# A hybrid decoder layer on one core: the second half of the sample's mLSTM states, moved from the mLSTM stage to VectorE's work beside the MLP

## The chip, the core and the metric

The kernel runs on 1 core of one Trainium2 chip. A time is device microseconds (us) of one execution; three runs were made of the kernel before, with a median of 2251.63 us (2251.58 to 2252.29).

## The reference, cut to what matters

One layer for 256 prompt tokens and 64 sample tokens (8 sequences of 8 tokens), all in fp32, with a width of 2048. Two token mixers read one input projection: an mLSTM with 4 heads (keys of 256, values of 512) and an HGRN2 recurrence with 8 heads. They are merged by gates, projected, normalised, and followed by an MLP of width 8192.

```python
h, C, n, m = _mlstm(q, k, v, ig, lf, C0, n0, m0)     # 4 heads, state C (256 x 512) each
...
mix = merged @ w_out
x1 = layernorm(alpha * x + mix)
hid = square(relu(x1 @ w_up))                        # 2048 -> 8192
y  = layernorm(alpha * x1 + hid @ w_down)            # 8192 -> 2048
```

Inside the mLSTM, each of the 8 sample sequences of each head brings a state of 256x512 and gives back a new one. The old state is also read by the queries:

```python
num   = einsum('bhts,bhsv->bhtv', s, v) + w_inter * einsum('bhtk,bhkv->bhtv', q, C)
w_end = exp(b[-1] - b + ig - m_new)
decay = exp(b[-1] + m - m_new)
C_new = decay * C + einsum('bhs,bhsk,bhsv->bhkv', w_end, k, v)
```

So a new state is the old one times one number (its sequence's decay) plus eight outer products, one for each token. A state's 256 rows are held as two halves of 128; the second half is what this change is about. The prompt's own states (one per head, from zero) are a different piece, computed at the very end.

## The kernel before, in words

**Weights.** Every large product is written as three products of halves: a factor is split into a high part (`xh`, `wh`) and the rest (`xl`, `wl`), both in the reduced fp32 form that TensorE reads, and xh·wh, xl·wh and xh·wl are added in a PSUM bank. There are 304 weight tiles of 128 output columns, each 16 steps of 128 input rows: 14,592 matmuls that take a 128x128 weight block and move 320 tokens past it. The tiles come in this order: 4 mLSTM heads (values, keys, queries), 8 HGRN heads, the output gates, the branch projections, the output projection `wo`, and then the MLP, four times 16 tiles of the up projection (`up`) and 16 of the down projection (`dn`).

**Units.** A unit is half a tile: 8 steps, 24 matmuls, 128x1024 weights (512 KB). Its way to TensorE has four links. `reload` (L527) issues the load on SP's DMA queue into one of three raw buffers `wr`. `prep` (L488) has ScalarE copy the high half (`A`, L342), into a free pair of buffers `wh`, `wl`. `low_half` (L515) has VectorE subtract it (L520), and spawns the load of the unit three further on into the same raw buffer. `give` (L601) takes the pair back when the unit's last matmul has been issued. There are three pairs `wh`, `wl`; from `wo` on to the end five wide pairs in the tile `bb` (`self.wx`) come to them, so eight in the MLP.

**Order of the side work.** Everything beside the weights is written as chains (Python generators) that ask for one instruction at a time, wait for events, or take and return buffers of a pool. `Sched` (L152) keeps an estimated time for each engine and steps the chains in the order of their priorities each time that a weight step has been placed (`pump`). An instruction is written when its chain's estimate is no more than 300 ns ahead of TensorE's; on ScalarE and VectorE the engine's own estimate must also be within 900 ns, and side matmuls are let in up to 900 ns at a time. The result is a fixed order for each engine; each engine then runs its own in order.

**The states before.** `m_states` (L1403) loads, for each head, 16 tiles of 128x512 (256 KB each): both halves of 8 sequences, in groups of four tiles, from a pool of 14 buffers `cb`, which are carved from other tiles of the stage (`rx`, `f` and others). `m_sample` (L1256) has two waves per head, each of four sequences with both halves, so eight tiles: the queries' product with the old states (eight matmuls, "q·C" below), and the outer products of the first half (`m_sums`, L1423: four matmuls `ra` of 32 rows by 512, one for each sequence, into four banks). `m_update` (L1432) then has VectorE form state times decay plus bank (L1441), spawns the stores, has TensorE make the second half's four sums into the same banks, and updates the second half. K and V for it come from `kst` and `vst`, copies of the sample's rows laid out in four blocks of 32 rows (`fourfold`, L1126, which reads K back from DRAM, 256 columns).

**The end.** `m_C` (L1194) computes the prompt's states from K and V that are loaded again from DRAM by POOL's queue. For heads 0 and 1 these go to buffers that `give` has set aside; for heads 2 and 3 (`late`) they go to the raw weight buffers `wr` once the last low half is done (`rest_ev`, L525), and are split by ScalarE (L342) and VectorE (L1918) into halves again. Meanwhile the last tile of the down projection is added by VectorE (L2240, L2241), and goes through the last layer norm's sums (L2065, L2066; earlier tiles L2053, L2054). TensorE adds these over rows by 24 matmuls of one column each, and multiplies the m_C halves before and after them.

## Time and profile before

| | before |
|---|---|
| time, median of 3 runs | 2251.63 us (2251.58 to 2252.29) |
| span of the profiled execution | 2246.3 us |
| TensorE (PE) busy | 2240.6 us, 16,218 matmul records |
| VectorE (DVE) busy | 1445.7 us, 64% |
| ScalarE (ACT) busy | 1012.3 us, 45% |
| GpSimd (POOL) busy | 21.0 us, 1% |
| DMA | 432.56 MB, mean 193 GB/s |

The profile is one execution of the kernel on the chip. The span goes from its first to its last instruction; the run's time has some 5 us around it. A row of an engine says what was busy; "idle before" is the time in which that engine stood still just ahead of an instruction, with the engine and the tile whose end released it. The PE row counts matmuls as busy while one is in the pipeline, so that 310 ns matmuls which start every 146 ns make an engine that is 100% busy. PEclk is the clock that TensorE was granted; it stands at 1.00 here. In rows of the timeline the first number is the start in us, the second the duration in us from the first to the last of a group ("x4").

### The profile page before, as it was taken

The page shows a single profiled execution, that of the slowest core. Times are in us where ns is not written, and L with a number is a line of the kernel's source. Part 1 is how long each engine was busy: PE and PEld are TensorE (multiplying, and loading weights), DVE is VectorE, ACT ScalarE, POOL GpSimd, SP SyncE. Part 2 cuts the span into 40 slices and gives each one's busy share as a digit, 9 for nine tenths or more (in the row PEclk, how much of TensorE's full clock was granted, in tenths as well). Part 3 has the DMA queues.
Part 4 walks back from the last instruction along what each step waited for, and adds up shares of the span by engine and source line. Part 5 has one row for each costly group of instructions (what it writes and reads, how often), then busy time and mean ns, then how long its engine had stood idle before and what let it go on. Part 6 is the DMA issues. An engine that isn't in the chain of part 4 may idle for free.

```text
span 2246.3 us, 40624 instructions
## 1 busy us (share of the span) xinstructions
PE 2240.6 (100%) x16218; PEld 2210.0 (98%) x16218; DVE 1445.7 (64%) x2584; ACT 1012.3 (45%) x1527; POOL 21.0 (1%) x53
## 2 busy tenths in 40 slices
PE   9999999999999999999999999999999999999999
PEld 9999999999999999999999999999999999999998
DVE  6768667888888887666556778444444444444566
ACT  5444444554555555444334456333432343234434
POOL 0000000000000000000000000000000000000001
PEclk9999999999999999999999999999999999999999
DMA  7998897776677754444446544444444444444554
GB/s 252 298 279 276 246 289 246 221 238 213 212 232 229 223 188 175 173 173 174 174 174 220 183 144 158 152 148 150 152 150 148 149 151 150 149 149 151 186 170 160
DMA packets 284982, 432.56 MB, mean 193 GB/s; under 512 B 136420, under 2 KB 181744, under 8 KB 284792
## 3 DMA queue, kind: packets, MB, share of 16 engines
q1 hardware_dynamic: 283832, 426.82, 57.3%
q0 software_dynamic: 960, 3.15, 0.5%
q8 instruction: 127, 2.08, 0.3%
q14 instruction: 63, 0.52, 0.1%
HBM read 380.52 MB, written 49.34 MB: 191 GB/s over the span
## 4 chain that ended last, share of the span: by engine, by line
PE 98%; DMA 1%; ACT 0%; SPq 0%; issue 0%; DVE 0%; POOL 0%; ACTq 0%; DVEq 0%; POOLq 0%
PE bank L348 98%; DMA wr<-wt 1%; DMA ra<-kD 0%; SPq L351 0%; ACT wh L342 0%; ACT f L342 0%; DVE wl L520 0%; DVE f L2066 0%; DVE f3m L2241 0%; DVE f2l L2065 0%; ACT misc L342 0%; DVE oS L1832 0%; ACT oS L342 0%; DVE f L966 0%; DVE f L1487 0%
## 5 line engine op out<-in xcount | busy, mean ns | idle before, releaser
L348 PE MATMUL bank<-xh,wh 128*128 128x320 f32 x2408 | 743.7, 310 | 0.0
L348 PE MATMUL bank<-xh,wl 128*128 128x320 f32 x2408 | 743.4, 310 | 0.0
L348 PE MATMUL bank<-xl,wh 128*128 128x320 f32 x2408 | 740.1, 308 | 0.0
L342 ACT ACTIVATE wh<-wr 128x1024 fp32r<-128x1024 f32 x424 | 448.5, 1058 | 588.3 <-PE bank L348 554.9
L520 DVE TENSOR_TENSOR wl<-wr,wh 128x1024 fp32r<-128x1024 f32 x423 | 516.8, 1222 | 293.2 <-ACT wh L342 288.6
L348 PEld LDWEIGHTS bank<-xh,wh 128*128 128x128 f32 x2408 | 452.6, 188 | 5.0 <-issue 3.9
L348 PEld LDWEIGHTS bank<-xl,wh 128*128 128x128 f32 x2408 | 452.1, 188 | 1.9
L348 PEld LDWEIGHTS bank<-xh,wl 128*128 128x128 f32 x2408 | 453.2, 188 | 0.0
L342 ACT ACTIVATE bb<-wr 128x1024 fp32r<-128x1024 f32 x181 | 191.8, 1061 | 353.9 <-PE bank L348 337.7
L520 DVE TENSOR_TENSOR bb<-wr,bb 128x1024 fp32r<-128x1024 f32 x179 | 219.0, 1224 | 157.4 <-ACT bb L342 157.3
L348 PE MATMUL bank<-rxb,bb 128*128 128x320 f32 x1264 | 287.7, 308 | 0.0
L348 PE MATMUL bank<-xh,bb 128*128 128x320 f32 (+1 forms) x1280 | 284.1, 309 | 0.0
L348 PE MATMUL bank<-ra,bb 128*128 128x320 f32 x1112 | 270.5, 308 | 0.0
L348 PE MATMUL bank<-ra,wh 128*128 128x320 f32 x968 | 259.4, 308 | 0.0
L348 PEld LDWEIGHTS bank<-xh,bb 128*128 128x128 f32 x1280 | 214.6, 188 | 0.0
L348 PEld LDWEIGHTS bank<-rxb,bb 128*128 128x128 f32 x1264 | 213.6, 188 | 0.0
L348 PE MATMUL bank<-xl,bb 128*128 128x320 f32 (+1 forms) x640 | 197.5, 309 | 0.0
L348 PEld LDWEIGHTS bank<-ra,bb 128*128 128x128 f32 x1112 | 190.7, 188 | 0.0
L348 PEld LDWEIGHTS bank<-ra,wh 128*128 128x128 f32 x968 | 172.5, 188 | 0.0
L348 PE MATMUL bank<-rxb,wl 128*128 128x320 f32 x520 | 160.3, 308 | 0.0
L348 PE MATMUL bank<-rxb,wh 128*128 128x320 f32 x520 | 160.3, 308 | 0.0
L348 PEld LDWEIGHTS bank<-xl,bb 128*128 128x128 f32 x640 | 120.2, 188 | 0.0
(343 smaller groups left out, 2132.7 us busy)
## 6 DMA issues: line engine op xcount, KB each, us to landing
wr<-wt SPq DMA_DIRECT2D x602, 512.0 KB, 3.2
rx<-C SPq DMA_DIRECT2D x34, 256.0 KB, 5.2
Cs<-rx SPq DMA_DIRECT2D x34, 256.0 KB, 5.4
f<-C SPq DMA_DIRECT2D x30, 256.0 KB, 5.1
Cs<-f SPq DMA_DIRECT2D x30, 256.0 KB, 4.5
f<-S SPq DMA_DIRECT2D x8, 512.0 KB
f3h<-S SPq DMA_DIRECT2D x8, 512.0 KB
Ss<-f SPq DMA_DIRECT2D x8, 512.0 KB, 4.8
```

The costliest lines, as they stand in the source:

```text
L342: return self.nc.scalar.activation(out, in_, func, **kw)
L348: self.nc.tensor.matmul(*a, **kw)
L520: self.V().tensor_tensor(lo, raw, hi.bitcast(F32), ALU.subtract)
```

## The change

The states are laid out anew in DRAM, with the two halves apart (`C0` and `Cs`: head, half, sequence, 128, 512). The first halves keep their path. Of the second halves only the read by the queries stays in the mLSTM stage. Their update is done later:

- `m_update` no longer makes the second group of sums. It posts the second halves' events and gives their buffers back when the wave's matmuls have been placed, without update or store; then come the four updates and stores of the first halves. `kst` holds 128 columns of K instead of 256.
- When tile 12 of the first 16 `up` tiles is reached, the five wide pairs are withdrawn as they come free (`retire`). Their place becomes the tile `fu`, with two buffers for V (4x512), five for states (1024) and two for K (80 columns).
- `m_late`, one head after the other: the sample's V rows are copied in DRAM from `vtD` to the new `vsD`, so that a token's 512 values lie together. Then eight loads of K (32 B per partition), two loads of V (each sequence's row repeated on 16 partitions, 1 MB in SBUF each), and a load of the decays. In this layout a sequence has 16 partitions and each partition holds 8 rows of a state.
- `m_late_part`, four to a head: load two of these 8 rows (512 KB), let ScalarE multiply by the decay, let VectorE add a token's V times the partition's K value (`scalar_tensor_tensor`, 128x512, 8 tokens x 2 rows = 16 instructions), and store.
- These 16 are of a new kind, "bg": one is written only where VectorE's estimate is at most 250 ns ahead of TensorE's.
- After head 3, `late_end` makes the same place into `bbx`, buffers for `m_C`. `give` returns a pair to the weights as long as units are left, so the weights have three pairs from there to the end.

```diff
 class Sched:
     PE_SIDE = 900.0
+    BG = 250.0
...
+            if kind == "bg":
+                if (r > now and c.eng != kind) or self.t["dve"] > now + self.BG:
+                    return False
+            elif kind == "pe":
...
-        self.kst = Pool([R.three(2, 256)])
+        self.kst = Pool([R.three(2, 128)])
...
+        if self.spare is not None and any(hl is w for w in self.wx):
+            self.retire(now, hl)
+        elif self.next_prep < len(UNITS):
             self.hl_free.append((now, hl))
...
+        elif kind == "up" and (h, c) == (12, 0):
+            self.spare = []
...
-            t = yield ("sp", 620, lambda: self.dma(cb, self.d["C0"][h, b, :, 512 * c:512 * c + 512]))
+            t = yield ("sp", 620, lambda: self.dma(cb, self.d["C0"][h, c, b]))
...
     def m_update(self, h, n, cbs, ps):
...
-        for i in (n, n + 4):
-            b, c = self.state(i)
-            if i > n:
-                yield ("pe", PE_4 + pe_r(512), lambda: self.m_sums(h, i, ps))
-            for x in range(4):
-                cb, p, bx = cbs[i - n + x], ps[x], b + x
+        b = self.state(n)[0]
+        for x in range(4):
+            yield post(m["inter"][n + 4 + x])
+            yield rel(self.cb, cbs[4 + x])
+        for x in range(4):
+            cb, p, bx = cbs[x], ps[x], b + x
...
+    def retire(self, now, hl):
+        self.spare.append(hl)
+        if len(self.spare) == len(self.wx):
+            A = self.Part(self.pool.tile([128, 10240], F32, name="fu", tag="f1"))
+            self.lv, self.lc, self.lk = (Pool([]) for _ in range(3))
+            self.lv.free = [(now, A.three(4, 512)) for _ in range(2)]
+            self.lc.free = [(now, A(1024)) for _ in range(5)]
+            self.lk.free = [(now, A(80)) for _ in range(2)]
+            for h in range(MH):
+                self.s.spawn(self.m_late(h), 8)
+
+    def m_late(self, h):
+        if h:
+            yield wait(self.late_ev[h - 1])
+        v = yield acq(self.lv, 2)
+        k = yield acq(self.lk)
+        at = lambda x: x.unsqueeze(1).to_broadcast([NB, 16, x.shape[1]])
+        yield ("sp", 620, lambda: self.dma(self.vsD[h].rearrange("t (j k) -> t j k", j=4), self.vtD[h][:, NP_:TOK].rearrange("j t k -> t j k")))
+        for t in range(NT):
+            x = self.kD[h][NP_:TOK, 128:256].rearrange("(b t) (d r) -> t b d r", t=NT, r=8)[t]
+            yield ("sp", 620, lambda: self.dma(k[:, 8 * t:8 * t + 8], x))
+        yield wait(self.later(3000))
+        for i in range(2):
+            x = self.vsD[h].rearrange("(b t) n -> b (t n)", t=NT)[:, 2048 * i:2048 * i + 2048]
+            yield ("sp", 620, lambda: self.dma(v[i].rearrange("p t n -> p (t n)"), at(x)))
+        yield ("sp", 620, lambda: self.dma(k[:, 64:65], at(self.scr[h, 704:712].unsqueeze(1))))
+        e = self.later(8000)
+        evs = [Ev() for _ in range(4)]
+        for q, x in enumerate(evs):
+            self.s.spawn(self.m_late_part(h, q, v, k, e, x), 9)
+        yield wait(*evs)
...
+    def late_end(self):
+        A = self.Part(self.pool.tile([128, 10240], F32R, name="bbx", tag="f1"))
+        for _ in range(MH):
+            yield rel(self.vx, A(2048))
+        for _ in range(2):
+            yield rel(self.kx, A(1024).rearrange("p (x s k) -> p x s k", x=2, s=2))
+
+    def m_late_part(self, h, q, v, k, e, ev):
+        of, to = (self.d[n][h, 1].rearrange("b (d r) v -> (b d) r v", r=8)[:, 2 * q:2 * q + 2] for n in ("C0", "Cs"))
+        c = yield acq(self.lc)
+        cb = c.rearrange("p (r v) -> p r v", r=2)
+        yield ("sp", 620, lambda: self.dma(cb, of))
+        yield wait(self.later(6000), e)
+        yield ("act", act(1024, False, 1), lambda: self.A(c, c, scale=k[:, 64:65]))
+        for t in range(NT):
+            for r in range(2):
+                x, y = v[t // 4][:, t % 4, :], k[:, 8 * t + 2 * q + r:8 * t + 2 * q + r + 1]
+                yield ("bg", dve(512, False, 1, 1), lambda: self.nc.vector.scalar_tensor_tensor(cb[:, r], x, y, cb[:, r], ALU.mult, ALU.add))
+        yield ("sp", 620, lambda: self.dma(to, cb))
+        yield wait(self.later(3000))
+        yield rel(self.lc, c)
+        yield post(ev)
```

In the changed kernel's rows the line of every matmul is L352 (L348 before), of every DMA on SP L355, of the low half L523 (L520), of a split for `m_C` L1987 (L1918), of the last tile's addition L2309 and L2310 (L2240 and L2241) and of its sums L2122, L2123, L2134 (L2053, L2054, L2065).

The order moves at three places. The first is TensorE's order in the first mLSTM head. Before, the second group of sums (`ra` 128x512, four row blocks into banks 89, 90, 85 and 86) stands alone between weight matmuls (`xh`, `xl` with `wh`, `wl`):

```order
L348 MATMUL bank_83<-xl,wh 128x320
L348 MATMUL bank_83<-xh,wl 128x320
L348 MATMUL bank_84<-xh,wh 128x320
L348 MATMUL bank_84<-xl,wh 128x320
L348 MATMUL bank_84<-xh,wl 128x320
L348 MATMUL bank_89<-ra 128x512
L348 MATMUL bank_90<-ra 128x512
L348 MATMUL bank_85<-ra 128x512
L348 MATMUL bank_86<-ra 128x512
```

Now the sums stand only behind a wave's q·C matmuls (the rows with `rx` and `f`, which are the state tiles); here is the second wave:

```order
L352 MATMUL bank_83<-xl,wh 128x320
L352 MATMUL bank_83<-xh,wl 128x320
L352 MATMUL bank_86<-misc,f_78 32x1 x4
L352 MATMUL bank_87<-rx,f_79 32x512 x6
L352 MATMUL bank_87<-f_79 32x512 x2
L352 MATMUL bank_89<-ra 128x512
L352 MATMUL bank_90<-ra 128x512
L352 MATMUL bank_85<-ra 128x512
L352 MATMUL bank_86<-ra 128x512
L352 MATMUL bank_83<-xh,wh 128x320
```

Of 16 groups of four such sums, 8 are left, each behind a wave of q·C.

The second place is the MLP, while one head's second halves are worked on. SP's queue held only the weights (`wr<-wt`) there before. Now, at the head after the first (`fu` is the new tile; `vsD`, `vtD`, `kD` and `scr` are in DRAM, `C` and `Cs` the old and new states):

```order
L355 DMA vsD_111<-vtD_127 256x1x128
L355 DMA wr<-wt 128x1024
L355 DMA fu<-kD_115 128x1x8 x4
L355 DMA wr<-wt 128x1024
L355 DMA fu<-kD_115 128x1x8 x4
L355 DMA wr<-wt 128x1024
L355 DMA fu<-vsD_111 128x1x2048
L355 DMA wr<-wt 128x1024
L355 DMA fu<-vsD_111 128x1x2048
L355 DMA fu<-scr 128x1x1
L355 DMA fu<-C 128x1024 x4
L355 DMA wr<-wt 128x1024 x8
```

Two loads of V and four of states stand between one weight load and the next. VectorE's order in the same stretch, over the end of one `dn` tile (L2310 adds its bank) and the start of the next:

```order
L523 TENSOR_TENSOR wl<-wr,wh 128x1024
L1517 SCALAR_TENSOR_TENSOR fu<-fu 128x512 x4
L523 TENSOR_TENSOR wl<-wr,wh 128x1024
L1517 SCALAR_TENSOR_TENSOR fu<-fu 128x512
L2310 TENSOR_TENSOR f3m<-f3m,bank_84 128x320
L1517 SCALAR_TENSOR_TENSOR fu<-fu 128x512 x2
L523 TENSOR_TENSOR wl<-wr,wh 128x1024
```

The updates (L1517) stand between one low half and the next, where there was nothing.

The third place is VectorE's order at the end, with the splits of heads 2 and 3 and the last tile. Before:

```order
L2053 TENSOR_TENSOR f2l<-f2l,f3m 128x320
L2054 TENSOR_TENSOR f2l<-f2l,f_78 128x320
L1918 TENSOR_TENSOR wh<-wr,wh 128x512
L1918 TENSOR_TENSOR wl<-wr,wl 128x512
L1918 TENSOR_TENSOR bb<-wr,bb 128x1024 x2
L2240 TENSOR_TENSOR f3m<-f3m,f2l 128x320
L2241 TENSOR_TENSOR f3m<-f3m,bank_84 128x320
L2065 TENSOR_TENSOR f2l<-f2l,f3m 128x320
```

Now:

```order
L2122 TENSOR_TENSOR f2l<-f2l,f3m 128x320
L2123 TENSOR_TENSOR f2l<-f2l,f_78 128x320
L1987 TENSOR_TENSOR wh<-wr,wh 128x512
L1987 TENSOR_TENSOR wl<-wr,wl 128x512
L1987 TENSOR_TENSOR bbx<-wr,bbx 128x1024
L2309 TENSOR_TENSOR f3m<-f3m,f2l 128x320
L1987 TENSOR_TENSOR bbx<-wr,bbx 128x1024
L2310 TENSOR_TENSOR f3m<-f3m,bank_84 128x320
L2134 TENSOR_TENSOR f2l<-f2l,f3m 128x320
```

L2309 stands ahead of the second split; L2310, which reads the last bank, is behind both as before. On TensorE all six of the first `m_C` product now stand ahead of the 24 one-column sums, where three did.

51 lines of the change are left out of this document (26 added, 25 removed).

## The prediction

> **What bounds the kernel now.** I read the page first (busy time, then the chain that ended last), then busy time by stretches of 100 us, then the tensor engine's timeline.
>
> ```profile
> span 2246.3 us, 40624 instructions
> PE 2240.6 (100%) x16218; PEld 2210.0 (98%) x16218; DVE 1445.7 (64%) x2584; ACT 1012.3 (45%) x1527; POOL 21.0 (1%) x53
> PE 98%; DMA 1%; ACT 0%; SPq 0%; issue 0%; DVE 0%; POOL 0%; ACTq 0%; DVEq 0%; POOLq 0%
> ```
>
> ```profile
> core 0: us, PE busy (x) PEld busy (x) DVE busy (x) ACT busy (x) POOL busy (x), PEclk, DMA share, GB/s
> 100.00:200.00 100.00, 100.00 (x723) 92.97 (x722) 73.61 (x139) 44.17 (x73) 0.00 (x0) 1.00 0.88 280
> 700.00:800.00 100.00, 100.00 (x859) 98.22 (x858) 90.79 (x244) 56.14 (x109) 0.37 (x1) 1.00 0.70 210
> 1400.00:1500.00 100.00, 100.00 (x685) 100.00 (x684) 45.94 (x52) 36.36 (x44) 0.00 (x0) 1.00 0.42 153
> ```
>
> TensorE has no idle time from the head to the end, at full clock, also where VectorE is 91% busy or the DMA engines 88%. Time can come only from matmuls that go away, and a new wait costs only if it reaches TensorE. In the MLP (third row) VectorE is free half the time; 685 matmuls in 100 us is 0.146 us for one, and 3.52 us for a unit of 24.
>
> **What is removed: 5.1 us.** Of the 16 groups of four matmuls that form a head's outer products, the change drops every second one, 8 groups. They are the ones that stand alone between weight matmuls:
>
> ```profile
> 97.66 0.31 PE L348 MATMUL bank<-xl,wh 128*128 128x320 f32 x1
> 97.81 0.31 PE L348 MATMUL bank<-xh,wl 128*128 128x320 f32 x1
> 98.05 0.51 PE L348 MATMUL bank<-ra 32*128 32x512 f32 x4
> 98.48 0.41 PE L348 MATMUL bank<-xh,wh 128*128 128x320 f32 x1
> 98.73 0.31 PE L348 MATMUL bank<-xl,wh 128*128 128x320 f32 x1
> ```
>
> From 97.81 to 98.73 are 0.92 to 0.93 us; without the group two ordinary steps of 0.146 would stand there, so one costs 0.635 us and eight cost 5.1. Bounds: the 0.43 us from 98.05 to 98.48 alone (3.4 in all), and the whole 0.93 (7.4); the step into and out of the group belongs to it, so I take 5.1. The Trainium skill ("TensorE: Matmul & The Clock Gate", Part 3 on packing small matmuls) has four 32-row matmuls run together in about the time of one, which would make a group 0.24 us, and the eight 1.9 us. The trace shows the four overlapping, but also the steps around them, and decides for 5.1.
>
> The 32 updates by VectorE and 32 stores that go from the mLSTM stage lie beside a busy TensorE and give nothing there. The narrower copy of K (half the bytes, conversions of 256 columns for 512) could shorten the only idle time of that stage:
>
> ```profile
> 88.59 0.31 PE L348 MATMUL bank<-misc,f 128*32 128x1 f32 x16
> 91.44 0.50 PE L348 MATMUL bank<-ra 32*128 32x512 f32 x1 [0.23 <-ACT misc L342]
> ```
>
> But the order puts head 0's group 9 matmuls (1.3 us) earlier, while the K copy lands when it did: 0 to 0.5 us either way, taken as 0.
>
> **A moved wait in that stage: taken as 0, at most 1 us.** The last two state loads of a head now wait for TensorE's reading of the tiles they overwrite, instead of for updates and stores. Behind them on SP's queue stand stores and the next weight load. The second q·C group follows the first after 57 weight matmuls (8.4 us) in heads 1 to 3, and after 36 (5.3 us) in head 0; before it was 87 throughout.
>
> ```profile
> wr<-wt SPq DMA_DIRECT2D x602, 512.0 KB, 3.2
> rx<-C SPq DMA_DIRECT2D x34, 256.0 KB, 5.2
> ```
>
> A state load lands 5.2 us after its issue; the tiles are read about 1 us into the second group. In heads 1 to 3 that leaves over 2 us, in head 0 about 1 after two issues. A late one would hold TensorE 1 us once.
>
> **What is added in the MLP: taken as 0.** 256 updates of 128x512 by VectorE, 16 scalings by ScalarE of 1.06 us, and per head a copy of V in DRAM, eight loads of K of 4 KB, two of V of 1 MB, a decay, four state loads and four stores of 512 KB. Paces, start to start:
>
> ```profile
> L342 ACT ACTIVATE wh<-wr 128x1024 fp32r<-128x1024 f32 x424 | 448.5, 1058 | 588.3 <-PE bank L348 554.9
> L520 DVE TENSOR_TENSOR wl<-wr,wh 128x1024 fp32r<-128x1024 f32 x423 | 516.8, 1222 | 293.2 <-ACT wh L342 288.6
> L1441 DVE SCALAR_TENSOR_TENSOR rx<-rx,f2a,bank 128x512 f32<-128x512 f32 x34 | 24.8, 742 | 4.4 <-PE bank L348 4.4
> ...
> 93.98 1.41 DVE L1441 SCALAR_TENSOR_TENSOR f<-f,f2a,bank 128x512 f32<-128x512 f32 x2
> 95.31 1.22 DVE L520 TENSOR_TENSOR wl<-wr,wh 128x1024 fp32r<-128x1024 f32 x1
> ...
> 2195.86 0.49 DVE L2053 TENSOR_TENSOR f2l<-f2l,f3m 128x320 f32<-128x320 f32 x1
> 2196.26 1.22 DVE L520 TENSOR_TENSOR bb<-wr,bb 128x1024 fp32r<-128x1024 f32 x1
> 2197.40 0.48 DVE L2054 TENSOR_TENSOR f2l<-f2l,f 128x320 f32<-128x320 f32 x1
> ```
>
> Two updates take 95.31 - 93.98 = 1.33, so 0.665 for one; a low half 1.14; a 320-column operation 0.40. The order gives a tile of the down projection two low halves, one addition and 6 or 7 updates: 2.28 + 0.40 + 6.5 x 0.665 = 7.0 us, against 7.04 of TensorE. VectorE is full while a head is worked on, 256 x 0.665 = 170 us in all, and the queue beside it holds what is at stake, the next weights' low half.
>
> Their cover shrinks at the same time. The high half starts when the unit whose buffers it takes is done, and 1.06 + 1.22, with 0.07 for the step between, 2.35 us later the low half is ready: with eight pairs of buffers 7 x 3.52 - 2.35 = 22 us ahead, with three 2 x 3.52 - 2.35 = 4.7. A weight load has 3 x 3.52 + 4.7 = 15.3 us from issue to first matmul, less 2.35 for the halves, so it may land 12.9 us after issue; now it takes 3.2. In a head's burst the worst-placed load finds ahead of it two V loads, four state loads and two weight loads: with itself 5.8 MB. At the rate of the MLP (153 GB/s at a share of 0.42 is 364 GB/s when full) that is 15.9 us, plus 1.8 of fixed landing time (3.2 less 0.52 MB at that rate), 17.7 after the first of them was issued and 10.7 after its own issue, two units later. Left of 12.9: 2.2 us. At the early stage's 280/0.88 = 318 GB/s, 18.2 + 1.8 = 20.0 leaves -0.1. So nothing or a fraction of a us per head; I take 0, since most of these packets are as long as those of the MLP.
>
> In a sentence of its own: the Trainium skill ("DMA: Bandwidth & Descriptors", Queues, rings and completion order) says that each DMA engine takes a ring's descriptors in order, by which a weight load does wait behind the whole burst; by it the sum stays as above, and no row here shows a burst of that size.
>
> **What comes back at the end: 2.0 us.** The last weights' lateness starts a chain:
>
> ```profile
> 2209.40 1.23 DVE L520 TENSOR_TENSOR bb<-wr,bb 128x1024 fp32r<-128x1024 f32 x1
> ...
> 2210.93 0.72 POOL L1206 DMA_DIRECT2D wr<-kD  x1 [2.82 <-DVE bb L520]
> 2211.65 2.98 POOL L1208 DMA_DIRECT2D wr<-vtD  x4
> ...
> 2217.93 2.01 ACT L342 ACTIVATE bb<-wr 128x1024 fp32r<-128x1024 f32 x2 [0.39 <-DMA wr<-vtD]
> ...
> 2219.03 2.36 DVE L1918 TENSOR_TENSOR bb<-wr,bb 128x1024 fp32r<-128x1024 f32 x2 [0.68 <-ACT bb L342]
> 2221.31 0.48 DVE L2240 TENSOR_TENSOR f3m<-f3m,f2l 128x320 f32<-128x320 f32 x1
> 2222.48 0.49 DVE L2241 TENSOR_TENSOR f3m<-f3m,bank 128x320 f32<-128x320 f32 x1 [0.69 <-PE bank L348]
> ```
>
> ```profile
> 2222.28 0.85 PE L348 MATMUL bank<-bb,wh 128*128 128x512 f32 x3
> 2223.55 0.37 PE L348 MATMUL bank<-misc,f2l 128*32 128x1 f32 x24 [0.41 <-DVE f2l L2065]
> 2224.36 1.20 PE L348 MATMUL bank<-bb,wh 128*128 128x512 f32 x4
> 2230.42 2.88 PE L348 MATMUL bank<-bb,wl 128*128 128x512 f32 x12
> ```
>
> The last unit starts at 2222.28 - 3.52 = 2218.76, and its low half ends at 2210.63, 8.1 us ahead: four buffers. With three it ends 4.7 us ahead (or less), so 3.5 later against TensorE. POOL's loads of K and V into the raw weight buffers wait for it; ScalarE and VectorE wait for those loads, and on VectorE's in-order queue the last tile's layer norm (L2241) stands behind the second split. It was free at 2221.31 + 0.40 = 2221.71 and waited for TensorE until 2222.48, a cover of 0.8. So layer norm starts 3.5 - 0.8 = 2.7 us later. On TensorE's queue the 24 one-column sums wait for it, and everything to the end is behind them. The changed order puts all six of the first product ahead of the sums, which fills 3 x 0.24 = 0.7 us of the gap (2.88 / 12 = 0.24). Cost 2.7 - 0.7 = 2.0. Bounds: 0, if the loads land so much sooner that the splits are done in time, and 2.7, if the filled gap is lost again in the short VectorE chain after the sums.
>
> **Sum.** 2246.3 - 5.1 + 0 + 0 + 2.0 = 2243.2 for the span. The runs' median of 2251.63 is 5.3 above the span; with the same 5.3 the time is 2248.5, that is 3.1 us or 0.14% less. A measurement of this kernel tells about 0.2%, 4.5 us, from no change: below 2247.1 is faster, above 2256.1 slower.
>
> **Rivals.** (a) The end holds, and the whole 5.1 stays: 2246.5, faster. For it speaks that the gap is only waiting, and loads land in 3 to 5 us; against it, that each link of the chain is shown above as waiting for the one before. (b) VectorE's full stretches stall TensorE, slower. The place is the low half behind a row of updates; it decides once 64 updates of a head lose more than the 2.2 us left, above 0.665 + 2.2/64 = 0.70 us for one. If updates that build on each other do not overlap and take their 0.745 (742 ns from end to end), a head loses 64 x 0.08 = 5.1, less 2.2 is 2.9; four heads 11.6: 2248.5 + 11.6 = 2260. For it speaks that the stretches are 100% full and that each update reads what the last but one wrote; against it, that there is one update between, and that the 91% of 700 to 800 us cost nothing. (c) Small stalls eat the gain: 1 us in head 0, 0.5 to 1 in each burst, some 3 to 5 together: 2251 to 2254, no change. (d) The copies or loads are late enough to block ScalarE and VectorE on a burst's data; that ends as (c) or (b), by size.
>
> **Chances.** Forecast 0.5, (a) 0.2, (b) 0.14, (c) with (d) 0.16. The likeliest's own range is 2247.2 to 2250; with (a) below and (c) and the beginning of (b) above, the range is 2246.0 to 2256.5. Faster 0.2, which is (a); same 0.64, the forecast with most of (c); slower 0.16, (b) and a remainder.
>
> **What would show it.** 8 groups of four 32-row matmuls left of 16, and the pace at the second q·C groups unbroken. VectorE near 100% in four stretches of 70 to 75 us between about 1455 and 1820 us, TensorE still at 100%; any idle time of TensorE there, put down to VectorE's low half, is (b). At the end the sums of the last layer norm should wait about 2.5 us for VectorE instead of 0.41; if they don't, it is (a). An idle TensorE at the second q·C group of head 0, put down to a state load, would be the first part of (c). The forecast is wrong if the span is below 2242 or above 2246.

## The result, and the profile after

The changed kernel takes 2320.16 us (median of 4 runs, 2319.18 to 2322.27) against 2251.61 us: 68.5 us more, ratio 1.0306 with a 95% interval of 1.0294 to 1.0318. The page of its profiled execution, head, clock and chain:

```profile
span 2320.4 us, 40806 instructions
PE 2250.0 (97%) x16186; PEld 2218.9 (96%) x16186; DVE 1583.8 (68%) x2808; ACT 1031.7 (44%) x1543; POOL 21.1 (1%) x53
PEclk9999999999999999999999999898989899999999
PE 92%; DMA 6%; DVE 1%; ACT 0%; issue 0%; SPq 0%; POOL 0%; ACTq 0%; DVEq 0%
PE bank L352 92%; DMA wr<-wt 4%; DMA fu<-vsD 2%; DVE wl L523 0%; ACT wh L346 0%; DMA wr<-vtD 0%; DMA f<-xw 0%; SPq L355 0%; DMA fu<-kD 0%; POOL wr L1215 0%; ACT bbx L346 0%; DVE f3m L2310 0%; DVE wh L780 0%; DVE f2l L2134 0%; DVE f3m L2309 0%
```

DMA has come into the chain (1% before, 6% now), by weights and by the loads of V, and the clock has four dents. What TensorE waited for, in us, times, and the longest:

```profile
PE bank L352 <- ACT wh L346: 57.7, 4, 16.9
PE bank L352 <- DVE f2l L2134: 4.1, 1, 4.1
PE bank L352 <- DVE wl L523: 2.1, 5, 0.7
```

The engine named is ScalarE's high half, but ScalarE itself waited. Its rows and TensorE's around the first of the four waits:

```profile
1449.38 1.06 ACT L346 ACTIVATE wh<-wr 128x1024 fp32r<-128x1024 f32 x1 [7.46 <-DMA wr<-wt]
1463.49 3.58 ACT L346 ACTIVATE fu<-fu 128x1024 f32<-128x1024 f32 x3 [13.06 <-DMA fu<-C]
1468.51 1.06 ACT L346 ACTIVATE wh<-wr 128x1024 fp32r<-128x1024 f32 x1 [1.43 <-DMA wr<-wt]
```

```profile
1469.62 0.64 PE L352 MATMUL bank<-rxb,wh 128*128 128x320 f32 x1 [14.35 <-ACT wh L346]
...
1471.31 0.47 PE L352 MATMUL bank<-rxb,wh 128*128 128x320 f32 x1
1471.57 0.47 PE L352 MATMUL bank<-ra,wh 128*128 128x320 f32 x1
...
1475.84 0.31 PE L352 MATMUL bank<-rxb,wl 128*128 128x320 f32 x1
1475.98 0.31 PE L352 MATMUL bank<-rxb,wh 128*128 128x320 f32 x1
```

The load behind the high half at 1468.51 was issued at 1448.11 and needed 20.4 us; 12.9 were to be had. It was also issued late: the low half that frees its raw buffer had ended at 1439.66, 8.4 us before. What SP's queue waited for in that time is V's first load, as it did eight times in the execution (us in all, times, longest; the same line of e17, an experiment below in which V loads fast, under it):

```profile
SPq L355 <- DMA fu<-vsD: 82.6, 8, 12.8
SPq L355 <- DMA fu<-vsD: 5.3, 5, 1.9
```

So in this burst V's loads delay the weight load twice, before its issue and on its way. TensorE stands 14.35 us, and then runs six more at half pace: a matmul starts every 0.27 us until 1475.84, then every 0.146. The same stretch in windows of 10 us:

```profile
1430.00:1440.00 10.00, 10.00 (x70) 10.00 (x69) 5.06 (x6) 4.01 (x5) 0.00 (x0) 1.00 0.55 128
1440.00:1450.00 10.00, 10.00 (x70) 10.00 (x69) 1.72 (x2) 1.69 (x2) 0.00 (x0) 1.00 1.04 188
1450.00:1460.00 10.00, 5.27 (x35) 4.80 (x33) 1.23 (x1) 0.44 (x1) 0.00 (x0) 0.94 1.00 152
1460.00:1470.00 10.00, 0.38 (x1) 0.38 (x2) 4.46 (x7) 4.93 (x5) 0.00 (x0) 0.50 0.60 211
1470.00:1480.00 10.00, 9.64 (x49) 9.24 (x49) 10.00 (x14) 3.56 (x5) 0.00 (x0) 0.71 0.52 164
1480.00:1490.00 10.00, 10.00 (x70) 10.00 (x69) 10.00 (x14) 3.18 (x3) 0.00 (x0) 1.00 0.63 211
```

The last three columns are clock, DMA share and GB/s. From 1440 to 1460 the DMA engines are fully busy and move 152 to 188 GB/s; the forecast had 364. In the last row VectorE is full, as forecast, and TensorE loses nothing.

When the first matmul of each unit starts, against before, splits the 74.2 us between the two spans into three pieces (they add up but for rounding): -4.0 us up to the MLP (fewer sums), +71.6 in the four bursts of loads (18.0, 17.9, 15.9 and 19.7), +6.7 after the last unit's start. Between the bursts the units keep step to 0.1 us. All further runs are read by these three pieces, always against the one profiled execution of before.

### The profile page after: what moved, and what is told of

It is laid out like the page before. It is cut to its first block, busy times and chain, and to the rows that moved or that the text cites. A ratio compares the mean times of both kernels' runs of the same rounds, so it can differ in the third digit from the quotient of the medians.

```text
span 2320.4 us, 40806 instructions
## 1 busy us (share of the span) xinstructions
PE 2250.0 (97%) x16186; PEld 2218.9 (96%) x16186; DVE 1583.8 (68%) x2808; ACT 1031.7 (44%) x1543; POOL 21.1 (1%) x53
## 4 chain that ended last, share of the span: by engine, by line
PE 92%; DMA 6%; DVE 1%; ACT 0%; issue 0%; SPq 0%; POOL 0%; ACTq 0%; DVEq 0%
PE bank L352 92%; DMA wr<-wt 4%; DMA fu<-vsD 2%; DVE wl L523 0%; ACT wh L346 0%; DMA wr<-vtD 0%; DMA f<-xw 0%; SPq L355 0%; DMA fu<-kD 0%; POOL wr L1215 0%; ACT bbx L346 0%; DVE f3m L2310 0%; DVE wh L780 0%; DVE f2l L2134 0%; DVE f3m L2309 0%
## 5 line engine op out<-in xcount | busy, mean ns | idle before, releaser
L523 DVE TENSOR_TENSOR wl<-wr,wh 128x1024 fp32r<-128x1024 f32 x563 | 687.6, 1221 | 383.2 <-ACT wh L346 378.4
L352 PE MATMUL bank<-xh,wh 128*128 128x320 f32 (+1 forms) x2896 | 895.4, 310 | 27.0 <-ACT wh L346 26.4
L352 PE MATMUL bank<-xh,wl 128*128 128x320 f32 (+1 forms) x2896 | 896.6, 310 | 1.4 <-DVE wl L523 1.4
L352 PE MATMUL bank<-xl,wh 128*128 128x320 f32 (+1 forms) x2896 | 892.4, 309 | 0.0
L352 PEld LDWEIGHTS bank<-xh,wh 128*128 128x128 f32 x2896 | 545.7, 189 | 31.2 <-ACT wh L346 27.4
L352 PEld LDWEIGHTS bank<-xh,wl 128*128 128x128 f32 x2896 | 546.6, 189 | 2.6 <-DVE wl L523 2.5
L352 PEld LDWEIGHTS bank<-xl,wh 128*128 128x128 f32 x2896 | 545.1, 188 | 1.9
L352 PE MATMUL bank<-ra,wh 128*128 128x320 f32 x1728 | 473.6, 310 | 16.9 <-ACT wh L346 16.9
L352 PE MATMUL bank<-rxb,wh 128*128 128x320 f32 x1024 | 317.2, 310 | 14.3 <-ACT wh L346 14.3
L352 PEld LDWEIGHTS bank<-ra,wh 128*128 128x128 f32 x1728 | 312.0, 189 | 17.2 <-ACT wh L346 17.2
L352 PE MATMUL bank<-rxb,wl 128*128 128x320 f32 x1024 | 317.0, 310 | 0.4 <-DVE wl L523 0.4
L1517 DVE SCALAR_TENSOR_TENSOR fu<-fu 128x512 f32<-128x512 f32 x256 | 179.4, 743 | 44.4 <-ACT fu L346 44.4
L352 PEld LDWEIGHTS bank<-rxb,wh 128*128 128x128 f32 x1024 | 193.4, 189 | 14.6 <-ACT wh L346 14.6
L352 PEld LDWEIGHTS bank<-rxb,wl 128*128 128x128 f32 x1024 | 193.3, 189 | 0.8 <-DVE wl L523 0.8
L352 PE MATMUL bank<-bb,wh 128*128 128x320 f32 x512 | 112.6, 309 | 0.0
L352 PE MATMUL bank<-ra,wl 128*128 128x320 f32 x352 | 109.4, 311 | 0.4 <-DVE wl L523 0.4
L352 PEld LDWEIGHTS bank<-bb,wh 128*128 128x128 f32 x512 | 85.7, 188 | 0.0
L352 PE MATMUL bank<-bb,wl 128*128 128x320 f32 x256 | 79.1, 309 | 0.0
```

What stands on the lines that cost most here:

```text
L352: self.nc.tensor.matmul(*a, **kw)
L523: self.V().tensor_tensor(lo, raw, hi.bitcast(F32), ALU.subtract)
L1517: yield ("bg", dve(512, False, 1, 1), lambda: self.nc.vector.scalar_tensor_tensor(cb[:, r], x, y, cb[:, r], ALU.mult, ALU.add))
```

## The experiments

| kernel | up to the MLP | bursts | end | span |
|---|---|---|---|---|
| changed kernel | -4.0 | 71.6 | 6.7 | 2320.4 |
| e1: V from distinct rows, one run of 128 | -5.3 | 0.2 | 4.6 | 2245.8 |
| e2: states contiguous | -4.8 | 71.6 | 7.0 | 2320.0 |
| e3: second halves left out | -4.0 | 0.0 | 4.3 | 2246.5 |
| e4: loads spread | -3.9 | 22.1 | 3.9 | 2268.4 |
| e5: spread, wide pairs given back | -4.7 | 28.1 | 0.5 | 2270.1 |
| e6: groups 16 by 8 (rows repeated) | -4.2 | 36.6 | 3.9 | 2282.6 |
| e9: e6, wide pairs given back | -4.5 | 35.0 | 0.4 | 2277.2 |
| e11: 16 copies of V, pairs back | -4.6 | 6.3 | 0.7 | 2248.7 |
| e13: 4 copies (32 by 4), pairs back | -2.9 | 6.1 | 0.7 | 2250.2 |
| e14: e13, loads spread | -5.1 | 0.0 | 0.5 | 2241.7 |
| e15: distinct rows, 8 by 16 | -5.1 | 72.3 | 4.6 | 2318.1 |
| e16: 2 copies (16 by 8), pairs back | -4.9 | 24.2 | 0.6 | 2266.1 |
| e17: one row for all 128 | -3.7 | 0.0 | 4.4 | 2246.9 |
| e18: distinct rows, 16 by 8 | -4.6 | 24.6 | 4.1 | 2270.3 |
| e19: V in loads of 16 partitions | -5.0 | 13.6 | 4.8 | 2259.7 |
| e20: e19, spread, pairs back | -2.8 | 0.0 | 0.3 | 2243.7 |
| e8, e12: before without second sums | -2.9, -1.5 | 0.0 | 0.3, 0.4 | 2243.6, 2245.1 |

The end of 2246.3 us of before is the zero of each column.

### Which transfer is slow: e1, e2, e3, e4

```diff
# e1
-            yield ("sp", 620, lambda: self.dma(v[i].rearrange("p t n -> p (t n)"), at(x)))
+            x = self.d["C0"][h, 0].rearrange("b (d r) v -> (b d) (r v)", r=4)[128 * i:128 * i + 128]
+            yield ("sp", 620, lambda: self.dma(v[i].rearrange("p t n -> p (t n)"), x))
# e2
-rearrange("b (d r) v -> (b d) r v", r=8)[:, 2 * q:2 * q + 2]
+rearrange("(q b) (d r) v -> q (b d) r v", q=4, r=2)[q]
# e3: the body of m_late is left out
# e4: after each V load, and before each state load
+            yield wait(self.later(14000))
+        yield wait(at)                  # 0, 7, 14, 21 us
```

> The two V loads of each head read 1 MB of distinct, contiguous DRAM (a stretch of the first-half states) instead of each sequence's row 16 times; packets stay 8 KB, everything else is as in the changed kernel. The second halves of the states are therefore computed with other numbers than V. The changed kernel's profiled execution splits into 2246.3 - 4.0 (fewer sums) + 71.5 (four bursts) + 6.6 (the end) = 2320.4. Theory A (many partitions reading the same DRAM rows slow every packet in flight): 8 KB packets go from 0.9 us to about 0.32, 4 KB packets from 0.46 to 0.16, a burst stalls TensorE by 0 to 2 us; span 2249 to 2257. Theory B (the state loads, 4 KB pieces 16 KB apart in DRAM, are what is slow): 4 KB packets stay near 0.46 and the bursts cost most of their 71.5; span 2300 to 2320. Theory C (volume alone: 5.8 MB in front of one weight load): no change, 2315 to 2322.

> State loads and stores of the late halves read and write 512 KB in one contiguous piece instead of 4 KB pieces 16 KB apart; V's loads stay as in the changed kernel. A partition then holds rows of another sequence than its V, K and decay belong to, so the second halves come out different. Theory A: no change, span 2310 to 2322. Theory B: bursts nearly free, span 2249 to 2257. Theory C: no change.

> The second halves of the states are left out: no V copy, no loads, scalings, updates or stores in the MLP. The five wide pairs are still taken from the weights, and the end is as in the changed kernel. All theories of the bursts: 2246.3 - 4.0 + 6.6 = 2248.9, with no wait of TensorE between 1430 and 2200 us. If three pairs of buffers alone were too few, TensorE would wait here as well and the span would be above 2250. If the end's 6.6 came from something that the bursts left behind, the span would be 2242 to 2245.

> Same work as the changed kernel, but the loads of a head are spread: four or five weight loads between the first and the second V load and again before the states, one or two between one state load and the next. Theory A: a V load still runs at its slow rate (12 to 14 us with 8 KB packets at 0.6 to 0.9 us), but a weight load beside it lands in 8 to 10 us, within the 12.9 it has: TensorE waits 0 to 1 us per head, span 2249 to 2253. Theory B: the same, as state loads come singly. Theory C: the same. If the rate of a single V load is so low that even one delays a weight load past 12.9 us, 4 to 8 waits of a few us remain and the span is 2260 to 2290.

e1 takes the whole stall away, e2 nothing: it is V's loads, not the states' (theory B falls), and not the volume alone (C falls). e1's windows of the same burst:

```profile
1430.00:1440.00 10.00, 10.00 (x70) 10.00 (x69) 4.56 (x5) 3.46 (x6) 0.00 (x0) 1.00 0.77 271
1440.00:1450.00 10.00, 10.00 (x71) 10.00 (x70) 7.00 (x9) 5.20 (x5) 0.00 (x0) 1.00 0.95 379
```

At 379 GB/s the burst fits: in e1's second burst the load of unit 418 waits 10.96 us, where the prediction's sum had 10.7, and 0.9 us of cover are left. e3 shows that three pairs of buffers by themselves stall nothing in the MLP; it was expected at 2248.9 and came at 2246.5, since its end costs 4.3 and not the changed kernel's 6.7. e4 was expected at 2249 to 2253, or at 2260 to 2290 if even one V load is too slow, and came at 2268.4: a single V load, with nothing else but weights in flight, still makes a weight load last 13.0 us (unit 390) or 17.8 (unit 395).

So far A, "reading a row 16 times is slow", looked right. It was wrong, as the next but one group shows: e1 had changed two things.

### The end, and the sums: e5, e8, e12

```diff
# e5 (on e4): after head 3 the five wide pairs return to the weights
+        self.wxv = [A(2048) for _ in range(5)]
+        self.wx = [(w[:, 0:1024], w[:, 1024:2048]) for w in self.wxv]
+        self.hl_free += [(self.s.t["pe"], x) for x in self.wx]
# e8, e12 (on the kernel before)
-            if i > n:
-                yield ("pe", PE_4 + pe_r(512), lambda: self.m_sums(h, i, ps))
```

> As e4 (spread loads), and after head 3 the five wide pairs go back to the weights, and the last buffers are set aside for the prompt's states by the rule of the kernel before. Theory of the end (the last low half comes 3.5 us later against TensorE with three pairs, and K, V, splits and layer norm follow): the end returns to that of before, the low half of the last unit 8.1 us ahead of its first matmul, and the span falls by the 4.3 us that e4 lost after its last unit, to 2264 (e4: 2268.4). Rival (the end is longer because the loads of K and V themselves take longer, or because of the order of the matmuls around the sums): the low half comes early but the end stays, 2267 to 2269.

> The kernel before, with only the second group of sums left out (8 groups of four matmuls): the second halves are updated with the first halves' sums, so their values differ; updates, stores and order of all else stay. By the prediction's step a group costs 0.635 us, 5.1 in all: span 2241.2. By the changed kernel's profile, which was 4.0 us ahead before the first burst: 2242.3. If the gain there came from other parts (narrower K, no second updates and stores in the stage), less than 3: above 2243.3.

> The kernel of e8 (before, with only the second group of sums left out, so that the second halves' values differ), timed, because its profiled span (2243.6) and its single time (2245.42 against 2251.39) gave different gains, 2.6 and 6.0 us. Eight groups at 0.635 us: 5.1 us, ratio 0.9977. Eight groups at 0.24 us: 1.9 us, ratio 0.9992.

e5's end is back to 0.5 us, and the last low half ends 8.1 us ahead of its unit again (4.6 in the changed kernel), so the end's loss is that of the buffers, as predicted; every kernel with three pairs to the end lost 3.9 to 7.0 there, every one with the wide pairs given back 0.3 to 0.7. (e5's span still missed the expected 2264 by 6, since its bursts cost 28.1 against e4's 22.1 with the same order of loads; that difference was not followed up.) The changed kernel's end, and that of e9:

```profile
2282.71 2.99 POOL L1215 DMA_DIRECT2D wr<-vtD  x4
2289.82 1.55 PE L352 MATMUL bank<-bbx 128*128 128x512 f32 x6
2290.66 2.00 ACT L346 ACTIVATE bbx<-wr 128x1024 fp32r<-128x1024 f32 x2 [4.67 <-DMA wr<-vtD]
2293.30 1.22 DVE L1987 TENSOR_TENSOR bbx<-wr,bbx 128x1024 fp32r<-128x1024 f32 x1
2294.43 0.48 DVE L2310 TENSOR_TENSOR f3m<-f3m,bank 128x320 f32<-128x320 f32 x1
2295.49 0.50 PE L352 MATMUL bank<-misc,f2l 128*32 128x1 f32 x24 [4.12 <-DVE f2l L2134]
```

```profile
2252.82 0.85 PE L352 MATMUL bank<-bbx,wh 128*128 128x512 f32 x3
2253.02 0.49 DVE L2317 TENSOR_TENSOR f3m<-f3m,bank 128x320 f32<-128x320 f32 x1 [1.13 <-PE bank L352]
2254.09 0.37 PE L352 MATMUL bank<-misc,f2l 128*32 128x1 f32 x24 [0.41 <-DVE f2l L2141]
```

Leaving out the eight groups gives a ratio of 0.9983 (0.9974 to 0.9992), 3.8 us, between 1.8 and 5.8: the 5.1 is inside, and so, at the edge, is 1.9. The 17 profiled kernels with the new mLSTM stage stand 2.8 to 5.3 us ahead when the MLP begins, median 4.6; the sums alone gave 2.9 (e8, whose span of 2243.6 is on the side where its expectation had other parts in the gain) and 1.5 (e12) in single profiles. All these stand against one execution of before, a short one: timed, e14 and e20 gain 6.5 and 7.4 us by their ratios (3.8 to 9.5 and 4.7 to 10.1). So the term was about right; its exact size these runs don't give, nor whether a part of the gain comes from elsewhere in the stage, the narrower K for one.

### The copies: e6, e9, e11, e13, e14

```diff
# e6, e9: sequence as the fast index of the partitions, for V, K, decays and states
-        at = lambda x: x.unsqueeze(1).to_broadcast([NB, 16, x.shape[1]])
+        at = lambda x: x.unsqueeze(0).to_broadcast([16, NB, x.shape[1]])
# e11: 16 copies of V's rows in DRAM, by doubling; e13, e14: 4 copies
+                yield ("sp", 620, lambda: self.dma(self.vsD[h][:, n:2 * n], self.vsD[h][:, 0:n]))
# e13, e14: the load
+ x.unsqueeze(1).to_broadcast([32, 4, 2048])
```

> The changed kernel with one edit: the sequence is the fast index of the partitions (partition = 8 x piece + sequence instead of 16 x sequence + piece) for V, K, decays and states alike. V's rows are still read 16 times each, in total the same bytes from the same addresses, but neighbouring partitions now read eight different rows. Theory A1 (the DMA engines work on neighbouring partitions at the same time, and so all read one row at once): packets go back towards 0.31 and 0.16 us, bursts cost little, span 2246 to 2255. Theory A2 (reading the same 64 KB over and over is slow in any order): no change, 2315 to 2322. The state loads now have 4 KB pieces in an order that jumps by 256 KB; if that is slow, 4 KB packets would rise in bursts where no V load is in flight.

> e6's partition order and e5's end (wide pairs given back), loads not spread. If A1 holds and the end is that of before: 2246.3 less 4.0 to 5.2, plus 0 to 2 of small waits: span 2241 to 2244.5, time 0.9970 to 0.9985 of before. If A2 holds: four bursts as in the changed kernel, 2246.3 - 4.0 + 71.5 = 2314.

> V's rows are written 16 times in DRAM ahead of time (one copy from the token rows, then four doublings, each reading distinct addresses, with two weight loads between), so that a V load reads 1 MB of distinct rows; partition order as in the changed kernel, bursts not spread; the end as in e5 (wide pairs given back). Theory A (reads of the same rows by many partitions): packets at 0.31 and 0.16 us as in e1, no wait of TensorE in the bursts; the end costs 0.4 as in e5 and e9; fewer sums give 4.0 to 5.2. Span 2246.3 - 4.0 (or 5.2) + 0.4 = 2241.5 to 2242.7, time 0.9965 to 0.999 of before. If the copies themselves (1 MB from DRAM to DRAM at a time) delay a weight load past 12.9 us, up to four waits of 1 to 5 us, span up to 2260.

> As e11 with only 4 copies of V's rows in DRAM, so each row is read by 4 neighbouring partitions. If a row's rate is what limits, 8 KB packets lie between e1's 0.31 and the changed kernel's 0.9 us, by proportion near 0.31 as soon as a row is asked for by 4 instead of 16: no waits, span 2241 to 2244. If two readers of a row already slow each other as much as sixteen, bursts stall as in the changed kernel: about 2314.

> e13 (4 copies of V's rows, wide pairs given back at the end) with the loads of a head spread as in e4: three weight loads between V loads, one or two between state loads. Theory A with volume as the second limit (at full rate a burst of 5.8 MB in front of a weight load uses up the 12.9 us to within a us or two, which is what e11 and e13 still waited for): no wait of TensorE in the MLP at all. Against the kernel before in the same runs: the sums' 3.7 us (e12's ratio 0.9983) less 0.4 to 0.7 at the end, so ratio 0.9985, 0.9975 to 0.9995. If the waits of e11 and e13 came from the copies or from something else than the burst's volume, 1 to 6 us remain: ratio 1.000 to 1.001 as in e11.

e6 and e9 came between the two expectations, half of the stall gone, which fits neither A1 nor A2 as told. e9 was timed: 1.0125 (1.0108 to 1.0142). With copies the stalls shrink to 6 us, and e13 showed that 4 readers of a row are as good as one. By theory A both were expected without waits, at 2241 to 2244, and came at 2248.7 and 2250.2; e11, timed, is no faster than before (ratio 1.0007, 0.9998 to 1.0017). What was left in them is volume: unit 417's weight load in e13 stood behind V's and the states' loads and lasted 14.3 us. e14 spreads them and has no wait of TensorE in the MLP; timed, it is 2244.17 us against 2251.13, ratio 0.9971 (0.9958 to 0.9983), 0.3% faster than before and a little more than expected (0.9985).

### Rows or grouping: e15, e16, e17, e18, e19, e20

Two things spoke against A. In the changed kernel V's packets start eight at a time, not sixteen (start in us and length in ns, from the trace's record of DMA packets):

```
1435.33/309 1435.35/309 1435.36/309 1435.37/309 1435.38/309 1435.39/309 1435.41/309 1435.42/309
1435.63/322 1435.65/346 1435.67/379 1435.67/359 1435.69/399 1435.70/414 1435.72/418 1435.72/464
1435.94/638 1435.99/599 1436.03/620 1436.04/607 1436.07/618 1436.10/619 1436.13/607 1436.17/620
```

And while V is alone in flight, half of the DMA engines are busy (last two columns: share and GB/s):

```profile
1436.00:1437.00 1.00, 1.00 (x9) 1.00 (x9) 0.13 (x1) 0.00 (x0) 0.00 (x0) 1.00 0.55 115
1437.00:1438.00 1.00, 1.00 (x9) 1.00 (x8) 0.49 (x1) 0.66 (x1) 0.00 (x0) 1.00 0.53 123
```

The load names its source as 8 sequences, each 16 times. e1 had named 128 rows, e6 16 groups of 8, e13 32 groups of 4. Theory D: the outermost count decides on how many engines a load runs.

```diff
# e15: x = ...rearrange("b (s r) v -> b s (r v)", r=4)[:, 16 * i:16 * i + 16]        distinct rows, 8 by 16
# e18: x = ....rearrange("(g s) n -> g s n", g=16)[:, 8 * i:8 * i + 8]               distinct rows, 16 by 8
# e16: x.unsqueeze(1).to_broadcast([16, 8, 2048])                                    2 copies, 16 by 8
# e17: x.to_broadcast([128, 2048])                                                   one row, 128 times
# e19, e20: eight loads of [16, 2048], one for each sequence, for one of [8, 16, 2048]
```

> As e1 (V loads read 1 MB of distinct rows; second halves come out with other numbers than V), but the 128 rows are named as 8 groups of 16 with an unequal step between groups, as the changed kernel's repeated rows are; e1 names them as one run of 128. Theory A (repeated rows are what is slow): as e1, no wait in the bursts, span 2244 to 2248. Theory D (a load whose outermost group count is 8 is done by 8 of the 16 DMA engines, and every transfer behind it waits for these 8): while a V load is alone in flight the DMA share is near 0.5, and bursts stall. By the lengths 2 MB of V on 8 engines take 32 x 0.31 = 10 us per head beside 3.8 MB on all, so 8 engines move 3.9 of the 5.8 MB: 3.9 / 0.206 = 19 us for the burst instead of 14, stalls of 4 to 8 us per head with the half clock after them, span 2260 to 2280. If both causes add, this run shows D alone and e6 A alone.

> As e13 with 2 copies of V's rows instead of 4: the load's outermost count becomes 16, and a row is still read 8 times, one time after the other by one engine. Theory D: all 16 engines work, DMA share near 1 while a V load is alone, bursts as in e13: waits of 1 to 1.5 us per head, span 2248 to 2252. Theory A: a row read 8 times in a row is still slow, 8 KB packets 0.5 to 0.9 us, stalls of 5 to 15 us per head, span 2270 to 2300.

> All 128 partitions of a V load read one and the same DRAM row (the first sequence's), named as one run of 128; all else is the changed kernel, so the second halves of sequences 1 to 7 come out with the first one's V. Theory A (repeated reads are slow), in its strongest form here: packets as slow as in the changed kernel or slower, stalls of 15 us and more per head, span 2300 or above. Theory D (it is the grouping of the access, 8 by 16, that puts the load on 8 engines and makes its packets slow): packets at 0.31 us, DMA share near 1, no wait in the bursts, span 2244 to 2249.

> V loads of distinct rows named as 16 groups of 8 with an unequal step (the second halves come out with other numbers than V); all else is the changed kernel. e16 had this grouping with each group's row repeated 8 times, 0.58 us per 8 KB packet on 16 engines. If the grouping makes packets slow: again 0.5 to 0.6 us, DMA share near 1 at 210 to 260 GB/s, waits of 3 to 5 us per head, span 2262 to 2275 (this kernel keeps the changed end, 4 us longer than e16's). If the repetition did it in e16: 0.31 us, no waits, span 2245 to 2250.

> One edit of the changed kernel: each V load is issued as eight loads of 16 partitions, one for each sequence, so that no access is grouped; same bytes from the same addresses, 14 more issues of 0.6 us on SP per head. Theory D: packets 0.31 us, the bursts cost nothing or 1 to 2 us per head (volume, and the extra issues on SP), the end as in the changed kernel: span 2246 to 2254. If a load of 16 partitions is as slow as a group of 16 in the changed kernel: 2310 and above.

> e19 with the loads of a head spread and the wide pairs given back before the end, as in e14, but without e14's copies in DRAM. Theory D and volume: no wait of TensorE in the MLP, as e14: ratio 0.997, 0.9955 to 0.9985. If the small loads hold SP's queue back enough to make weight loads late: 1 to 6 us, ratio 0.9985 to 1.0005.

e17 reads one row 128 times and is as fast as e1, its windows at the same place:

```profile
1436.00:1437.00 1.00, 1.00 (x9) 1.00 (x8) 0.48 (x1) 0.00 (x0) 0.00 (x0) 1.00 1.00 410
1437.00:1438.00 1.00, 1.00 (x9) 1.00 (x8) 0.17 (x1) 0.32 (x1) 0.00 (x0) 1.00 1.00 414
```

e15 reads no row twice and stalls like the changed kernel:

```profile
1435.00:1436.00 1.00, 1.00 (x9) 1.00 (x8) 0.09 (x1) 0.00 (x0) 0.00 (x0) 1.00 0.55 106
1436.00:1437.00 1.00, 1.00 (x9) 1.00 (x8) 0.49 (x1) 0.71 (x1) 0.00 (x0) 1.00 0.44 131
```

For loads of 128 partitions, repeating a row costs nothing, and the grouping costs all. The median 8 KB packet of V in the MLP, and the median of the 4 KB packets (weights, states) that start while one of V's is in flight, from the packet records:

```
V load named as                  kernel   8 KB, us   4 KB beside, us
128 rows, distinct               e1       0.31       0.16
128 times one row                e17      0.31       0.16
32 groups of 4, repeated         e13      0.31       0.16
16 groups of 8, distinct         e18      0.60       0.23
16 groups of 8, repeated         e16      0.58       0.27
8 groups of 16, distinct         e15      0.73       0.40
8 groups of 16, repeated         changed  0.87       0.46
16 partitions, repeated          e19      0.85       0.35
```

Eight groups cost twice over: half of the engines, and packets of 0.6 us instead of 0.31 with V alone, 0.9 with the rest beside. Sixteen groups have all engines busy (e18: 262 and 176 GB/s from 1437 to 1439 us), but slow packets still, and 24 us of stall; e16 so came at 2266.1, between the 2252 of D and the 2270 of A. e15's price had been set at 4 to 8 us per head from the engine count alone; it was 18, because the slow packets were not in it. Why the packets of 8 and 16 groups are slow is not settled. e19 is no clean test of it: its loads have no grouping, and 16 packets go to 16 neighbouring partitions at once and take 0.85 us. That points to the side that is written rather than the one that is read, but no run separates the two. Alone in flight, e19's V comes at 131 GB/s (1439 to 1440 us), no faster than with 8 groups. What its pieces change is the order: they are issued from 1432.05 to 1450.06 with four weight loads between them, where the changed kernel issues its two V loads within 4 us. e19 was expected at up to 2254 and came at 2259.7: its bursts still cost 13.6 instead of 71.6, and there SP's queue, busy with the many issues and their waits, gave out unit 394's weight load only at 1457.22, 10.6 us after the one before.

e20, with the loads spread and the wide pairs given back, has nothing left in bursts and end:

```profile
span 2243.7 us, 40857 instructions
PE 2236.4 (100%) x16186; PEld 2208.3 (98%) x16186; DVE 1583.8 (71%) x2808; ACT 1029.0 (46%) x1543; POOL 21.0 (1%) x53
```

Timed it is 2243.67 us (2242.89 to 2245.47) against 2250.35, ratio 0.9967 (0.9955 to 0.9979): the change as meant, without the two losses.

## Why the prediction was wrong, point by point

**Removed, 5.1 us: about right.** 4.0 in the changed kernel's profile, 2.8 to 5.3 in its relatives; the sums alone 3.8 when timed (1.8 to 5.8), and 1.5 and 2.9 in profiles. The prediction's other price, 1.9 us, is at the edge of the timed interval and not excluded.

**Moved wait in the mLSTM stage, 0: right.** The loss is nowhere: TensorE's waits before the MLP are 2.1 us in all, 1.2 before, and both are in the gain above.

**Added in the MLP, 0: wrong, by 71.6 us.** The step that failed is the landing time of the worst-placed weight load, 5.8 MB at the rate of the MLP (364 GB/s when full), 10.7 us after its issue. Amount and order and the 12.9 us that it may take were right, and e1 measured 10.96 us for the 10.7; but the rate was taken from transfers of another shape. In the changed kernel the same bytes went at 152 to 188 GB/s, since V's loads ran on 8 engines with slow packets, and the load took 20.4 us in the first burst. The sum also took it for granted that the load is issued on time, and it went out 8.4 us late, because SP's queue waited for V (82.6 us over the eight V loads, 5.3 in e17). That was so in the first two bursts; in the third and fourth the load that TensorE waited for went out at most 1.5 us late and took 26.1 and 29.7 us. Whether an earlier issue would have brought an earlier landing, no run shows. The prediction named "most of these packets are as long as those of the MLP" as its reason; the length was right and said nothing on the rate. The Trainium skill ("DMA: Bandwidth & Descriptors", Rules for kernel authors) has the number of engines: the slowest dimension that isn't 1 sets it, and an outermost dimension below 16, a repeated one too, confines a load to at most that many. The trace agrees (8 packets at a time, share 0.53 to 0.55). The slow packets came on top. The diff showed the shape, [8, 16, 2048], and it was not read. Rows repeated 16 times look like the cause at first sight and are not.

On top of each wait of 12 to 17 us came about 3 us that no term had: a unit of 24 matmuls took 6.80 us instead of 3.52 after the first. The trace shows the half pace, from 1469.62 to 1475.84, and a clock of 0.50 in the window from 1460 to 1470. The Trainium skill ("TensorE: Matmul & The Clock Gate", Part 1) has the clock at half after some 3.4 us without work, until it has been busy as long. The measurements differ in both figures: here the half pace lasted 6.2 us of work, and by the clock records of these runs every wait of 2.3 us or more in the MLP and at the end came with 3.4 us or more at half clock, and so did about half of those between 1.0 and 2.2 us (several have a second wait, of 0.7 us, close behind).

**The end, 2.0 us: right place, too small.** It was 6.7 in the changed kernel, 3.9 to 7.0 in all with three pairs. The link that was worked out held to 0.1 us: POOL's loads of V start 7.1 us ahead of the last tile's end (2282.71 to 2289.82), 10.6 before. The next one did not: the 3.5 us were passed on, and ScalarE's split came 5.2 us later, since these loads took 8.0 us from issue to split in this execution against 6.3 (6.5 to 7.0 in e1, e3, e4 and e6). So layer norm was 4.4 us later and not 2.7, and TensorE stood 4.1 us, where it was 0.4 before. That is 3.7 of the 6.7; for the other 3.0, which no term had, it ran on at a lower clock in the next 10 us (the column ahead of the last two):

```profile
2294.00:2299.00 5.00, 3.50 (x55) 3.02 (x56) 3.86 (x12) 2.01 (x6) 0.00 (x0) 0.60 0.01 3
2299.00:2304.00 5.00, 5.00 (x21) 4.23 (x20) 3.35 (x6) 2.47 (x4) 0.61 (x1) 0.72 0.38 139
```

**From span to time, 5.3 us: wrong.** Later executions of both kernels have 1.7 to 1.9 us outside the span. The profiled execution of before was simply one of the shorter ones (spans of before: 2246.1 to 2253.8), so 3.5 of the 5.3 were spread between runs and should have widened the range instead.

**The rivals.** (b), VectorE's full stretches, did not occur: it was full as said, and the low halves, once each burst's wait was over, stayed 3.4 to 4.0 us ahead in the changed kernel's first stretch and 1.2 or more in the others. It was near, though: in e1, where nothing stalls, most of those of the fourth stretch were ready only 0.3 to 0.8 us ahead. (d), loads late enough to block, was the right kind, but was given no price of its own, and the range ended where a full DMA rate ended. (a) was wrong; the end did not hold.

## What to carry to other kernels

Read the shape of an added load, not only its bytes: count the outermost dimension of its source, and if it is 8 or 16, write it as one run of rows or in 32 groups, or issue it by pieces with other loads between them (the pieces themselves were no faster here). What a slow load costs is not its own time but that of whatever shares its queue, so price the worst-placed transfer behind it against its slack, its issue as well as its landing, and take a rate only from a load of the same shape. A wait of TensorE of 4 us or more cost 2.5 to 3.9 us on top of its length here, and buffers that an early stage lends out have to be back before the end.

## What the runs showed of the hardware that had not been expected

A DRAM row read by all 128 partitions costs no more than 128 rows (0.31 us per 8 KB packet, 410 GB/s). A load of the same bytes named as 8 groups ran at 106 to 143 GB/s when alone, as 16 groups at 164 to 279, as 32 groups at 303 to 393 and as one run at 401 to 414; in pieces of 16 partitions at 131. And a slow load slows the others: 4 KB packets of weights and states beside it took 0.46 us instead of 0.16, and SP's queue stood 82.6 us for it. Half the clock came with some waits of TensorE as short as 1.0 us, and with all from 2.3 us on.
